# The first FFN's first chunks computed without the shift, which is added to them later

## The chip, the cores and the metric

One Trainium2 (trn2) chip; the kernel runs on one core. The metric is the device time of one execution in microseconds (us). A core has TensorE (PE; its weight loads are listed as PEld), VectorE (DVE), ScalarE (ACT), GpSimd (POOL) and SyncE (SP). Here SP and POOL issue nearly all loads, which land in SBUF through 16 shared DMA engines. Each engine, and each queue of loads, works through its instructions in order.

## The reference

One step of a two-layer network on T = 384 tokens (128 context, 256 latent) of width 1024. Each layer is a half-step FFN, a mixer, and a second half-step FFN, so the kernel has six stages s = 0..5; s = 0 and 3 are the first FFNs. What matters here is the start of the first FFN:

```python
mod = silu(cond) @ w_ada + b_ada          # nine vectors of 1024 per layer, one set per kind of token
shift, scale, gate = mod[0], mod[1], mod[2]
h = rmsnorm(x, g[0]) * (1.0 + scale) + shift
g, u = split(h @ w_ffn_in)                # w_ffn_in: 1024 x 5632 (2816 for g, 2816 for u)
x = x + 0.5 * gate * ((silu(g) * u) @ w_ffn_out)
```

cond is one vector for the context tokens and one for the latent tokens, so shift and scale have two columns. rmsnorm multiplies each token by one number r. Thus h @ w = r * ((x * g[0] * (1 + scale)) @ w) + shift @ w, and the last product is one number per output column and kind of token.

## The kernel before, in words

All matrices are fp32. Each is split in a high part (a cast on ACT, L470) and the rest (a subtraction on DVE, L471), and each product takes three matmuls: high x high, high x low, low x high (`mm3`, L474; lines L475, L476, L477). Activations lie feature by feature: xT is 8 k-blocks of 128 features by 384 tokens.

**An FFN** (`ffn`, L562) has 22 chunks f of 128 columns of g and 128 of u. A chunk takes two slabs (`ffn_slab`, L555; `wslab`, L460) of 512 KB, one for k-blocks 0 to 3 and one for 4 to 7, each loaded by two issues of 256 KB on SP's queue (L466). It runs 24 mm3 products of 384 columns into pg and 24 matmul triples in the same manner into pu, 48 matmuls in all, then SiLU, the product with u and a split into aH and aL. After the 22 chunks the out part (po) multiplies them by w_ffn_out. The slabs' raw tiles have 5 buffers (tag X), the high parts 4 and the low parts 4; the chunks' sums have 4 banks of PSUM (tag pw).

**Two forms of the left factor.** `mod_chunk` (L502) makes h itself for one k-block, split in hH and hL: on DVE two products t = xT * am * r (L508) and two subtractions (L512), on ACT two additions of the shift. `raw_chunk` (L520) makes x * am only, am = g[0] * (1 + scale), without r, and puts the two columns of the shift behind the 384 tokens (L526, L531), so that the same matmuls yield shift @ w in columns 384 and 385 (TR = 386). A chunk that uses raw factors multiplies by r afterwards and adds those two numbers (L581 to L587). N_RAW says how many chunks of each FFN do that; for s = 0 it is the first two, since r is late.

**The modulation vectors.** `ada_first` (L297) forms shift and scale of stage 0, in four calls of 256 columns each: four loads of 512 KB on SP's queue (L309), 32 small matmuls with 32-column weights (each seen as two passes in the trace), a copy on ACT, a transposition on PE, an addition, am. It is called before everything else of the FFN, with two `raw_chunk` calls after each call, and the slabs of f = 0 and f = 1 are loaded after the calls i = 0 (k-blocks 0 to 3) and i = 2 (k-blocks 4 to 7). Its tiles come from the tags K (3 buffers) and X. All other vectors, 1024 columns each, are groups (s, p) of a stream (`Stream`, L394; `ada_group`, L343): p = 0 shift, 1 scale, 2 gate. A group has 8 steps; a step loads 512 KB on POOL's queue (L354; tag AX, 3 buffers) and either multiplies on PE (4 matmuls, L368) or accumulates on DVE (two instructions of 128x1024, L360 and L362; at the group's end 8 matmuls with a block of ones add up the partitions, L378, then a transposition, L379). The order is (0,2), (1,0), (1,1), (1,2), ...; ADA_F says how many DVE steps are spread over an FFN's chunks and over its out part, for s = 0 20 and 12.

**The order of the work.** A list scheduler places each engine's instructions ahead of time: by default in program order, a ready instruction before one that is not; slabs' splits get a lead of 60 instructions. `behind` puts one instruction after another on its engine. `late_loads` (L221) issues 18 small parameter loads on POOL's queue once the last raw factor is there (L531).

Of the kernel before, what the change touches and what calls it, by code (L numbers as in the profile page):

```python
# [11 lines left out]
F32 = mybir.dt.float32  # L12
# [24 lines left out]
ADA_F = [[20, 12], None, [24, 12], [20, 16], None, [8, 0]]  # L37
ADA_M = [14, 0]

N_RAW = [2, None, 2, 2, None, 2]  # L40
# [44 lines left out]
def hybrid_step_kernel(  # L85
# [211 lines left out]
    def ada_first(i):  # L297
# [3 lines left out]
        for q in range(2):  # L301
            xs = []
            for g in range(2):
                if (i + q) % 2 == 0:
                    x = kp.tile([P, HALF_K, 256], F32, name="adax", tag="K")
                else:
                    x = wp.tile([P, HALF_K, 256], F32, name="adax", tag="X")
                rows = w_ada[0, q * HALF_K * P : (q + 1) * HALF_K * P, g * D + 256 * i : g * D + 256 * i + 256]
                nc.sync.dma_start(x, rows.rearrange("(k p) n -> p k n", p=P))  # L309
                xs.append(x)  # L310
            for kk in range(HALF_K):
                k = q * HALF_K + kk
                for g in range(2):
                    for j in range(2):
                        r0 = 64 * g + 32 * j
                        mm(
                            bank[r0 : r0 + 32, 0:P],
                            sc[:, k, :],
                            xs[g][:, kk, j * P : (j + 1) * P],
                            start=(k == 0),  # L320
                            stop=(k == KD - 1),
                        )
        sb = mp.tile([P, 512], F32, name="adasb", tag="adasb", bufs=1)
        nc.scalar.copy(sb[:, 0:P], bank[:, 0:P])
        ps = PS("psada", "p2")
        nc.tensor.transpose(ps[:, 0:P], sb[:, 0:P], ident)
        m = slice(2 * i, 2 * i + 2)
        V.tensor_tensor(
            md[:, 0:16, :].rearrange("p (g m) c -> p g m c", g=2)[:, :, m, :],
            ps[:, 0:P].rearrange("p (g j c) -> p g j c", g=2, j=2)[:, :, :, 0:2],  # L330
            vC[0][:, 0:16].rearrange("p (g m) -> p g m", g=2)[:, :, m].unsqueeze(3).to_broadcast([P, 2, 2, 2]),
# [3 lines left out]
            am[:, m, :],  # L335
            md[:, KD + 2 * i : KD + 2 * i + 2, :],
            1.0,
            g_norm(0, 0)[:, m].unsqueeze(2).to_broadcast([P, 2, 2]),
# [4 lines left out]
    def ada_group(s, p, on_dve):  # L343

        l, i = divmod(s, 3)
# [3 lines left out]
        bias = vC[l][:, i * 24 + KD * p : i * 24 + KD * p + KD]  # L349
        accs = [K5(f"ada{c}") for c in range(2)] if on_dve else None  # L350
        bank = None if on_dve else PS("adaps", "pa")
        for k in range(KD):
            x = wp.tile([P, 1024], F32, name="adax", tag="AX", bufs=3)
            nc.gpsimd.dma_start(x, w_ada[l, k * P : (k + 1) * P, c0 : c0 + D])  # L354
            if on_dve:
                x = x.rearrange("p (h n) -> p h n", h=2)
                for c in range(2):
                    w = sc[:, k, c : c + 1]
# [6 lines left out]
            else:  # L365
                x = x.rearrange("p (m a j) -> p a m j", m=KD, a=4)
                for a in range(4):
                    ins = mm(bank[32 * a : 32 * a + 32, 0:256], sc[:, k, :], x[:, a], start=(k == 0), stop=(k == KD - 1))  # L368
                    if norm_last["pe"] is not None:
                        behind(ins, norm_last["pe"])  # L370
            yield
        sb = mp.tile([P, 512], F32, name="adasb", tag="adasb", bufs=1)
        if on_dve:
# [5 lines left out]
            V.transpose(out=sb, in_=bank)  # L379
            src = sb.rearrange("p (c m j) -> p m c j", c=2, m=KD)[:, :, :, 0]  # L380
# [11 lines left out]
    norm_last = {"dve": None, "pe": None}  # L392
# [28 lines left out]
    ada = Stream([(0, 2)] + [(s, p) for s in range(1, 3 * DEPTH) for p in range(3)])  # L421
# [98 lines left out]
    def raw_chunk(s, k):  # L520
# [873 lines left out]
```

## Time and profile before

| | us |
|---|---|
| median of 3 runs (1579.45 to 1580.15) | 1580.09 |
| the profiled execution, device time | 1580.6 |
| its span, first to last instruction | 1578.8 |
| share of PE in the chain that ended last | 88% |
| mean granted TensorE clock | 0.991 |

The span is what the trace covers; 1.8 us of the profiled execution lie around it, and it is 0.5 us over the median. A row of a view by lines reads: line, engine, operation, out<-in by the program's names, shape, count | busy us, mean ns of one | idle time before. A row in order of time reads: start, duration (of the whole merged piece), engine, line, operation, count, and in brackets the idle time before it and what ended it. The duration of one matmul in these rows is its latency; successive ones start about half as far apart, because they are pipelined.

### The profile page before, as it was taken

The page shows a single profiled execution, that of the slowest core. Times are in us where ns is not written, and L with a number is a line of the kernel's source. Part 1 is how long each engine was busy: PE and PEld are TensorE (multiplying, and loading weights), DVE is VectorE, ACT ScalarE, POOL GpSimd, SP SyncE. Part 2 cuts the span into 40 slices and gives each one's busy share as a digit, 9 for nine tenths or more (in the row PEclk, how much of TensorE's full clock was granted, in tenths as well). Part 3 has the DMA queues.
Part 4 walks back from the last instruction along what each step waited for, and adds up shares of the span by engine and source line. Part 5 has one row for each costly group of instructions (what it writes and reads, how often), then busy time and mean ns, then how long its engine had stood idle before and what let it go on. Part 6 is the DMA issues. An engine that isn't in the chain of part 4 may idle for free.

```text
span 1578.8 us, 24260 instructions
## 1 busy us (share of the span) xinstructions
PE 1527.9 (97%) x9118; PEld 1441.2 (91%) x9118; DVE 1113.6 (71%) x2068; ACT 746.6 (47%) x1376; POOL 103.4 (7%) x194
## 2 busy tenths in 40 slices
PE   7999999999889999999999999999978999999998
PEld 5899999998668999999999999999857699999998
DVE  5888586587677988578578866777967789443332
ACT  4533332469577633333363333325975864333221
POOL 1202010001100001001000200110000000000000
PEclk9999999999999999999999999999989999999999
DMA  9978576523531587566537866674231046444341
GB/s 304 248 205 228 158 231 196 147 80 115 185 106 37 146 245 211 161 207 225 171 97 215 238 187 193 203 238 121 64 92 37 15 134 201 130 117 128 116 145 35
DMA packets 291034, 249.02 MB, mean 158 GB/s; under 512 B 11554, under 2 KB 273159, under 8 KB 290917
## 3 DMA queue, kind: packets, MB, share of 16 engines
q1 hardware_dynamic: 270224, 175.94, 38.2%
q0 software_dynamic: 20368, 71.34, 14.8%
q8 instruction: 71, 1.16, 0.3%
q14 instruction: 47, 0.38, 0.1%
q10 hardware_dynamic: 324, 0.20, 0.1%
HBM read 245.17 MB, written 2.27 MB: 157 GB/s over the span
## 4 chain that ended last, share of the span: by engine, by line
PE 88%; DVE 4%; ACT 4%; issue 2%; DMA 1%; POOL 0%; ACTq 0%; DVEq 0%; POOLq 0%
PE po L475 9%; PE po L476 9%; PE po L477 9%; PE pg L475 8%; PE pg L477 8%; PE pg L476 8%; PE pu L475 8%; PE pu L477 8%; PE pu L476 8%; PE psw L476 1%; PE psg L891 1%; PE psw L475 1%; PE psw L477 1%; PE adaps L378 1%; ACT gate L143 1%
## 5 line engine op out<-in xcount | busy, mean ns | idle before, releaser
L471 DVE TENSOR_TENSOR wl<-wx,wh 128x1024 fp32r<-128x1024 f32 (+2 forms) x332 | 385.4, 1163 | 302.8 <-ACT wh L470 294.3
L470 ACT CAST wh<-wx 128x1024 fp32r<-128x1024 f32 (+2 forms) x332 | 333.2, 1005 | 448.5 <-PE po L476 237.3
L362 DVE SCALAR_TENSOR_TENSOR ada<-adax,sc,ada 128x1024 f32<-128x1024 f32 x196 | 244.2, 1280 | 17.8 <-DMA adax<-in_w_ada_dram 17.4
L475 PE MATMUL po<-aH,wh 128*128 128x384 f32 x704 | 239.7, 341 | 0.0
L477 PE MATMUL po<-aH,wl 128*128 128x384 f32 x704 | 237.7, 338 | 0.0
L476 PE MATMUL po<-aL,wh 128*128 128x384 f32 x704 | 237.2, 337 | 0.0
L475 PE MATMUL pg<-hH,wh 128*128 128x384 f32 x640 | 216.9, 339 | 0.0
L475 PE MATMUL pu<-hH,wh 128*128 128x384 f32 x640 | 216.2, 338 | 0.0
L477 PE MATMUL pg<-hH,wl 128*128 128x384 f32 x640 | 215.9, 337 | 0.2 <-DVE wl L471 0.2
L477 PE MATMUL pu<-hH,wl 128*128 128x384 f32 x640 | 215.6, 337 | 0.0
L476 PE MATMUL pu<-hL,wh 128*128 128x384 f32 x640 | 215.5, 337 | 0.0
L476 PE MATMUL pg<-hL,wh 128*128 128x384 f32 x640 | 215.4, 337 | 0.0
L143 ACT ACTIVATE sg<-pg 128x384 f32<-128x384 f32 x80 | 39.4, 493 | 206.5 <-PE pg L477 206.5
L475 PEld LDWEIGHTS po<-aH,wh 128*128 128x128 f32 x704 | 132.4, 188 | 3.9 <-issue 2.1
L476 PEld LDWEIGHTS po<-aL,wh 128*128 128x128 f32 x704 | 132.2, 188 | 0.5 <-issue 0.5
L477 PEld LDWEIGHTS po<-aH,wl 128*128 128x128 f32 x704 | 132.2, 188 | 0.0
L354 POOL DMA_DIRECT2D adax<-in_w_ada_dram x128 | 68.1, 533 | 892.3 <-DVE ada L360 466.5
L475 PEld LDWEIGHTS pg<-hH,wh 128*128 128x128 f32 x640 | 120.2, 188 | 2.5 <-issue 2.1
L477 PEld LDWEIGHTS pg<-hH,wl 128*128 128x128 f32 x640 | 120.1, 188 | 0.6 <-DVE wl L471 0.5
L476 PEld LDWEIGHTS pg<-hL,wh 128*128 128x128 f32 x640 | 120.2, 188 | 0.0
L475 PEld LDWEIGHTS pu<-hH,wh 128*128 128x128 f32 x640 | 120.2, 188 | 0.0
L477 PEld LDWEIGHTS pu<-hH,wl 128*128 128x128 f32 x640 | 120.1, 188 | 0.0
(327 smaller groups left out, 2425.9 us busy)
## 6 DMA issues: line engine op xcount, KB each, us to landing
wx<-in_w_ffn_in_dram SPq DMA_DIRECT2D x352, 256.0 KB, 4.1
adax<-in_w_ada_dram POOLq DMA_DIRECT2D x128, 512.0 KB, 4.9
wx<-in_w_ffn_out_dram SPq DMA_DIRECT2D x80, 512.0 KB, 3.9
wx<-in_w_in_dram SPq DMA_DIRECT2D x28, 512.0 KB, 3.8
adax<-in_w_ada_dram SPq DMA_DIRECT2D x16, 512.0 KB, 7.7
wx<-in_w_ffn_out_dram SPq DMA_DIRECT2D x16, 256.0 KB, 3.3
wx<-in_w_out_dram SPq DMA_DIRECT2D x8, 512.0 KB, 3.9
wx<-in_w_out_dram SPq DMA_DIRECT2D x16, 256.0 KB, 2.7
```

The lines of the kernel that those rows point to most:

```text
L143: ins = nc.scalar.activation(out, in_, func, **kw)
L354: nc.gpsimd.dma_start(x, w_ada[l, k * P : (k + 1) * P, c0 : c0 + D])
L362: ins = V.scalar_tensor_tensor(accs[c], x, w, accs[c], ALU.mult, ALU.add)
L378: mm(bank[32 * a : 32 * a + 32, 256 * c : 256 * c + 256], cm(C_ONE, n1=32), x[:, a], start=True, stop=True)
L470: nc.scalar.copy(h[:, 0:nk, 0:ncol], x[:, 0:nk, 0:ncol])
L471: V.tensor_tensor(lo[:, 0:nk, 0:ncol], x[:, 0:nk, 0:ncol], h[:, 0:nk, 0:ncol].bitcast(F32), ALU.subtract)
L475: mm(out, wh, xh, start=first, stop=False)
L476: mm(out, wh, xl, start=False, stop=False)
L477: last_mm[0] = mm(out, wl, xh, start=False, stop=last)
L891: mm(ps[:, 0:TG], wg[:, wi, :], xcs[ch], start=True, stop=True)
```

## The change

For s = 0, `ada_first` loads and forms the scale only: two loads per call in place of four, 16 matmuls in place of 32. `raw_chunk` no longer writes the shift's two columns for s = 0; `raw_cols` does that later. The shift becomes group (0,0) of the stream, on PE, and its first load on POOL's queue waits for the last matmul of `ada_first`; the three loads that POOL issued at the very start are no longer there. Chunks f = 0 to 3 ("late" chunks) run on raw factors over the 384 tokens alone; DVE multiplies their two sums by r into tiles of SBUF that are kept. The 8 steps of (0,0) stand two by two after pg and after pu of f = 2 and f = 3. Behind f = 3 come `raw_cols` for the 8 k-blocks, `late_loads` and the 8 calls of `mod_chunk`. Chunk f = 4 uses the raw factors with the two columns, f = 5 to 21 use h. Group (0,1), which had been the scale's, now forms shift @ w_ffn_in for the columns of f = 0 to 3: 8 steps on DVE, each loading 512 KB of w_ffn_in on POOL's queue, then 8 summing matmuls and a transposition; `late_shift` adds the result to the kept tiles, does SiLU, product and split. The DVE steps, 28 in place of 20, are spread over f = 5 to 21.

```diff
-ADA_F = [[20, 12], None, [24, 12], [20, 16], None, [8, 0]]
+ADA_F = [[28, 12], None, [24, 12], [20, 16], None, [8, 0]]
...
-N_RAW = [2, None, 2, 2, None, 2]
+N_RAW = [1, None, 2, 2, None, 2]
+
+N_LATE = 4
...
@@ -299,63 +301,73 @@
-            xs = []
-            for g in range(2):
-                if (i + q) % 2 == 0:
-                    x = kp.tile([P, HALF_K, 256], F32, name="adax", tag="K")
-                else:
-                    x = wp.tile([P, HALF_K, 256], F32, name="adax", tag="X")
-                rows = w_ada[0, q * HALF_K * P : (q + 1) * HALF_K * P, g * D + 256 * i : g * D + 256 * i + 256]
-                nc.sync.dma_start(x, rows.rearrange("(k p) n -> p k n", p=P))
-                xs.append(x)
+            if q == 0:
+                x = kp.tile([P, HALF_K, 256], F32, name="adax", tag="K")
+            else:
+                x = wp.tile([P, HALF_K, 256], F32, name="adax", tag="X")
+            rows = w_ada[0, q * HALF_K * P : (q + 1) * HALF_K * P, D + 256 * i : D + 256 * i + 256]
+            nc.sync.dma_start(x, rows.rearrange("(k p) n -> p k n", p=P))
...
+        norm_last["scale"] = ins
...
-        nc.tensor.transpose(ps[:, 0:P], sb[:, 0:P], ident)
-        m = slice(2 * i, 2 * i + 2)
+        nc.tensor.transpose(ps[:, 0:64], sb[0:64, 0:P], cm(C_ID, 0, 64, 0, 64))
...
+        late = (s, p) == (0, 1)
+        on_dve = on_dve or late
+        first_load = []
         for k in range(KD):
             x = wp.tile([P, 1024], F32, name="adax", tag="AX", bufs=3)
-            nc.gpsimd.dma_start(x, w_ada[l, k * P : (k + 1) * P, c0 : c0 + D])
+            if late:
+                win = w_ffn_in[0, 0, k * P : (k + 1) * P, :].rearrange("p (g n) -> p g n", g=2)
+                nc.gpsimd.dma_start(x.rearrange("p (g n) -> p g n", g=2), win[:, :, 0 : N_LATE * P])
+            else:
+                ins = nc.gpsimd.dma_start(x, w_ada[l, k * P : (k + 1) * P, c0 : c0 + D])
+                if (s, p) == (0, 0):
+                    if k == 0:
+                        tc.add_manual_dep(ins.ins, norm_last["scale"].ins.name, sync, reason="order of the loads")
+                        first_load.append(ins)
+                    else:
+                        behind(ins, first_load[0])
             if on_dve:
                 x = x.rearrange("p (h n) -> p h n", h=2)
                 for c in range(2):
-                    w = sc[:, k, c : c + 1]
+                    w = md[:, k, c : c + 1] if late else sc[:, k, c : c + 1]
...
                 for a in range(4):
                     ins = mm(bank[32 * a : 32 * a + 32, 0:256], sc[:, k, :], x[:, a], start=(k == 0), stop=(k == KD - 1))
-                    if norm_last["pe"] is not None:
-                        behind(ins, norm_last["pe"])
+                    behind(ins, last_mm[0])
...
+            if late:
+                late_shift(sb.rearrange("p (c g f j) -> p c g f j", c=2, g=2, f=N_LATE))
+                return
...
-    ada = Stream([(0, 2)] + [(s, p) for s in range(1, 3 * DEPTH) for p in range(3)])
+    ada = Stream([(s, p) for s in range(3 * DEPTH) for p in range(3)])
...
         h, lo = LT("rH", (P, TR), F32R), LT("rL", (P, TR), F32R)
         for j, sl in SEG:
             act(h[:, sl], xT[:, k, sl], AF.Copy, scale=am[:, k, j : j + 1])
-        V.tensor_copy(h[:, T:TR], md[:, k, :])
         for j, sl in SEG:
             V.scalar_tensor_tensor(
                 lo[:, sl], xT[:, k, sl], am[:, k, j : j + 1], h[:, sl].bitcast(F32), ALU.mult, ALU.subtract
             )
+        raws.setdefault(s, []).append((h, lo))
+        if s:
+            raw_cols(s, k)
+
+    def raw_cols(s, k):
+        md, _ = mods[s]
+        h, lo = raws[s][k]
+        V.tensor_copy(h[:, T:TR], md[:, k, :])
         norm_last["raw"] = V.tensor_tensor(lo[:, T:TR], md[:, k, :], h[:, T:TR].bitcast(F32), ALU.subtract)
-        raws.setdefault(s, []).append((h, lo))
...
+    late_acts = []
+
+    def late_shift(b):
+
+        for f in range(N_LATE):
+            sg, su_ = late_acts[f]
+            for j, sl in SEG:
+                act(sg[:, sl], sg[:, sl], AF.Silu, bias=b[:, j, 0, f, 0:1])
+            for j, sl in SEG:
+                V.scalar_tensor_tensor(sg[:, sl], su_[:, sl], b[:, j, 1, f, 0:1], sg[:, sl], ALU.add, ALU.mult)
+            late_acts[f] = split(sg, "a", pool=LT)
...
-            raw = f < N_RAW[s]
-            xs, n = (raws[s], TR) if raw else (hs, T)
+            late = s == 0 and f < N_LATE
+            raw = not late and f < N_RAW[s] + (N_LATE if s == 0 else 0)
+            xs, n = (raws[s], T) if late else (raws[s], TR) if raw else (hs, T)
             for ps, o in ((pg, 0), (pu, P)):
                 for k in range(KD):
                     h, lo = slabs[k // HALF_K]
                     w0 = slice(o, o + P)
                     kk = k % HALF_K
-                    mm3(ps[:, 0:n], h[:, kk, w0], lo[:, kk, w0], *xs[k], k == 0, k == KD - 1)
+                    xh, xl = (x[:, 0:n] for x in xs[k])
+                    mm3(ps[:, 0:n], h[:, kk, w0], lo[:, kk, w0], xh, xl, k == 0, k == KD - 1)
+                if late and f >= 2:
+                    ada.step(2)
+            if late:
+                late_acts.append((S("sg"), S("su")))
+                for x, ps in zip(late_acts[f], (pg, pu)):
+                    V.tensor_tensor(x, ps[:, 0:T], r, ALU.mult)
+                acts.append(None)
+                if f == N_LATE - 1:
+                    for k in range(KD):
+                        raw_cols(0, k)
+                    late_loads(norm_last["raw"])
+                    hs = [mod_chunk(0, k, r) for k in range(KD)]
+                continue
...
-            if f >= 2:
+            f0 = N_LATE + 1 if s == 0 else 2
+            if f >= f0:
                 n = ADA_F[s][0]
-                ada.step(n * (f - 1) // (KF - 2) - n * (f - 2) // (KF - 2), True)
+                ada.step(n * (f + 1 - f0) // (KF - f0) - n * (f - f0) // (KF - f0), True)
...
         ada.until(s, 2)
+        acts[0 : len(late_acts)] = late_acts
+        late_acts.clear()
...
-    hs = [mod_chunk(0, k, r) for k in range(KD)]
-    late_loads(norm_last["raw"])
+    hs = None
```

## Rows read from the trace of the kernel before

**Rows 1.** The page: busy time by engine, and the chain by engine

```profile
PE 1527.9 (97%) x9118; PEld 1441.2 (91%) x9118; DVE 1113.6 (71%) x2068; ACT 746.6 (47%) x1376; POOL 103.4 (7%) x194
...
PE 88%; DVE 4%; ACT 4%; issue 2%; DMA 1%; POOL 0%; ACTq 0%; DVEq 0%; POOLq 0%
```

**Rows 2.** Busy time by stretch: us, each engine's busy time (instructions), granted clock, DMA share, GB/s

```profile
0.00:22.54 22.54, 12.83 (x98) 8.58 (x98) 8.41 (x24) 9.01 (x18) 4.10 (x9) 1.00 0.99 319
22.54:58.58 36.04, 31.58 (x291) 23.97 (x292) 24.55 (x79) 19.26 (x42) 3.11 (x6) 0.91 0.91 260
58.58:229.60 171.02, 170.79 (x993) 168.49 (x993) 137.10 (x194) 67.94 (x93) 24.22 (x45) 1.00 0.76 212
229.60:329.00 99.40, 99.40 (x580) 95.93 (x579) 62.12 (x105) 36.55 (x59) 4.24 (x8) 1.00 0.57 170
```

**Rows 3.** PE in order of time: start, us, line, tile, count

```profile
22.54 0.45 PE L475 MATMUL pg<-rH,wh 128*128 128x386 f32 x1
...
50.47 1.07 PE L316 MATMUL ada<-adax,sc 128*32 128x128 f32 x28
...
53.91 0.45 PE L475 MATMUL pg<-rH,wh 128*128 128x386 f32 x1 [0.44 <-ACT rH L143]
...
58.58 0.34 PE L475 MATMUL pg<-hH,wh 128*128 128x384 f32 x1
```

**Rows 4.** PE in order of time, end of the first FFN's chunks

```profile
230.27 0.33 PE L475 MATMUL po<-aH,wh 128*128 128x384 f32 x1
```

**Rows 5.** DMA from 0 to 58.58 us: bytes; issues, KB each, us to landing

```profile
DMA packets 19247, 16.54 MB, mean 282 GB/s; under 512 B 793, under 2 KB 18469, under 8 KB 19242
...
adax<-in_w_ada_dram SPq DMA_DIRECT2D x16, 512.0 KB, 7.7
...
adax<-in_w_ada_dram POOLq DMA_DIRECT2D x3, 512.0 KB, 8.5
```

**Rows 6.** What SP's queue waited for, 0 to 80 us: total, times, longest

```profile
SPq L466 <- DVE wl L471: 19.7, 8, 8.3
SPq L309 <- PE ada L316: 8.2, 3, 4.3
```

**Rows 7.** PE by line, 0 to 58.58 us: count, busy us, mean ns

```profile
L316 PE MATMUL ada<-adax,sc 128*32 128x128 f32 x256 | 13.6, 314 | 2.2 <-DVE acc L439 1.3 <-DMA adax<-in_w_ada_dram 0.9
```

**Rows 8.** Chain of waits: one group's summing on PE

```profile
127.08 1.00 PE adaps L378 x16
```

**Rows 9.** PE in order of time, modulation steps on PE in the first mixer

```profile
403.27 0.64 PE L368 MATMUL adaps<-adax,sc 128*32 128x256 f32 x8 [3.67 <-DMA adax<-in_w_ada_dram]
```

**Rows 10.** Busy time by stretch around two dips of the granted clock

```profile
40.00:45.00 5.00, 2.62 (x28) 1.70 (x32) 4.80 (x13) 3.45 (x8) 0.00 (x0) 0.81 1.10 346
45.00:50.00 5.00, 5.00 (x30) 3.74 (x22) 1.37 (x4) 0.91 (x2) 0.00 (x0) 0.50 1.20 293
...
400.00:405.00 5.00, 0.64 (x8) 0.16 (x8) 4.44 (x12) 3.52 (x7) 1.17 (x3) 1.00 0.98 345
405.00:410.00 5.00, 4.84 (x20) 2.48 (x21) 1.25 (x5) 1.82 (x7) 1.63 (x3) 0.66 1.06 363
```

**Rows 11.** POOL's loads of w_ada: ns of one issue; us from issue to landing

```profile
L354 POOL DMA_DIRECT2D adax<-in_w_ada_dram x128: 530/530/657, 2.5 to 1333.6; - x128
...
DMA to landing us min/median/max: 3.7/4.9/9.7
```

**Rows 12.** DVE by line and shape, 20 to 58.58 us

```profile
L512 DVE SCALAR_TENSOR_TENSOR hL<-ht,md,hH 128x256 fp32r<-128x256 f32 x8 | 3.9, 482 | 0.3 <-ACT hH L143 0.3
...
L512 DVE SCALAR_TENSOR_TENSOR hL<-ht,md,hH 128x128 fp32r<-128x128 f32 x8 | 2.8, 350 | 0.2
...
L526 DVE CAST rH<-md 128x2 fp32r<-128x2 f32 x8 | 1.3, 164 | 0.0
```

**Rows 13.** DVE by line, 58.58 to 227 us

```profile
L362 DVE SCALAR_TENSOR_TENSOR ada<-adax,sc,ada 128x1024 f32<-128x1024 f32 x43 | 53.8, 1281 | 7.7 <-DMA adax<-in_w_ada_dram 7.6
L471 DVE TENSOR_TENSOR wl<-wx,wh 128x1024 fp32r<-128x1024 f32 x42 | 51.2, 1222 | 21.8 <-ACT wh L470 21.7
```

More of the change, by code (lines that the diff above doesn't have):

```diff
@@ L311, in ada_first @@
+            rows = w_ada[0, q * HALF_K * P : (q + 1) * HALF_K * P, D + 256 * i : D + 256 * i + 256]
+            nc.sync.dma_start(x, rows.rearrange("(k p) n -> p k n", p=P))
             for kk in range(HALF_K):
                 k = q * HALF_K + kk
[L313 to L322, printed above, removed]
+                for j in range(2):
+                    ins = mm(
+                        bank[32 * j : 32 * j + 32, 0:P],
+                        sc[:, k, :],
+                        x[:, kk, j * P : (j + 1) * P],
+                        start=(k == 0),
+                        stop=(k == KD - 1),
+                    )
@@ L323, in ada_first @@
+        norm_last["scale"] = ins
         sb = mp.tile([P, 512], F32, name="adasb", tag="adasb", bufs=1)
-        nc.scalar.copy(sb[:, 0:P], bank[:, 0:P])
+        nc.scalar.copy(sb[0:64, 0:P], bank[0:64, 0:P])
         ps = PS("psada", "p2")
-        nc.tensor.transpose(ps[:, 0:P], sb[:, 0:P], ident)
-        m = slice(2 * i, 2 * i + 2)
+        nc.tensor.transpose(ps[:, 0:64], sb[0:64, 0:P], cm(C_ID, 0, 64, 0, 64))
+        m = slice(KD + 2 * i, KD + 2 * i + 2)
         V.tensor_tensor(
-            md[:, 0:16, :].rearrange("p (g m) c -> p g m c", g=2)[:, :, m, :],
-            ps[:, 0:P].rearrange("p (g j c) -> p g j c", g=2, j=2)[:, :, :, 0:2],
-            vC[0][:, 0:16].rearrange("p (g m) -> p g m", g=2)[:, :, m].unsqueeze(3).to_broadcast([P, 2, 2, 2]),
+            md[:, m, :],
+            ps[:, 0:64].rearrange("p (j c) -> p j c", j=2)[:, :, 0:2],
+            vC[0][:, m].unsqueeze(2).to_broadcast([P, 2, 2]),
@@ L334, in ada_first @@
         V.scalar_tensor_tensor(
-            am[:, m, :],
-            md[:, KD + 2 * i : KD + 2 * i + 2, :],
+            am[:, 2 * i : 2 * i + 2, :],
+            md[:, m, :],
             1.0,
-            g_norm(0, 0)[:, m].unsqueeze(2).to_broadcast([P, 2, 2]),
+            g_norm(0, 0)[:, 2 * i : 2 * i + 2].unsqueeze(2).to_broadcast([P, 2, 2]),
             ALU.add,
@@ L390, in ada_group @@
             V.tensor_scalar(md[:, m, :], md[:, m, :], 0.5, None, op0=ALU.mult)
-    norm_last = {"dve": None, "pe": None}
+    norm_last = {"dve": None}
     class Stream:
@@ L496, in norm_stat @@
         for n_, sq in enumerate(acc["sq"]):
-            norm_last["pe"] = mm(ps[:, 0:T], cm(C_ONE), sq, start=(n_ == 0), stop=(n_ == len(acc["sq"]) - 1))
+            mm(ps[:, 0:T], cm(C_ONE), sq, start=(n_ == 0), stop=(n_ == len(acc["sq"]) - 1))
         return rsqrt_newton(ps[:, 0:T], T, 1.0 / D, acc["t"])
```

## The prediction, made before the changed kernel ran

> **What bounds the kernel now.** I read the page first: PE is busy for 97% of the span and holds 88% of the chain that ended last [rows 1], so a saving counts only where PE itself does less, or where PE waits. The busy times by stretch show where it waits. From 58.58 us on, PE is busy in 170.79 of 171.02 us of the first FFN's remaining chunks, and then without a gap through the out part; before 58.58 us it is not, and the DMA engines are (share 0.99 and 0.91, 319 and 260 GB/s) [rows 2]. PE in order of time gives the marks: the first FFN matmul starts at 22.54 us, the last call of `ada_first` ends at 51.54 us, the matmuls that hang on it begin at 53.91 us, and f = 2 starts at 58.58 us [rows 3]; the out part begins at 230.27 us [rows 4]. So f = 0 and 1, two chunks of 48 matmuls, end only at 58.58 us. By then 16.54 MB have been moved, of which 16 loads of 0.52 MB on SP's queue for shift and scale (8.4 MB) and three on POOL's for the gate (1.6 MB); one takes 7.7 us and 8.5 us to land [rows 5]. The stretch is bound by bytes, with some turns of buffers: SP's queue waited 19.7 us for the slabs' splits and 8.2 us for the small matmuls [rows 6].
>
> A chunk's pace follows from the marks. Between 58.58 and 230.27 us lie 171.7 us: 20 chunks, two summings of a group on PE (L378; 1.00 us each [rows 8], 1.2 us with the slower start of the matmuls behind), and 0.8 us of small things. So a chunk takes (171.7 - 2.4 - 0.8) / 20 = 8.42 us.
>
> **The change, part by part.** All sums are made on the profiled execution (span 1578.8 us, 1580.6 us in all, 0.5 us over the median of 1580.09); the difference is carried to the median. I compute E, the time at which f = 0 and 1 are done, and then the start of the out part.
>
> *Removed: half of `ada_first`'s loads and matmuls, and POOL's three early loads.* Ahead of the last scale load there were 8.4 MB of modulation, 2.1 MB of slabs, 1.6 MB of tokens and 1.6 MB from POOL; now there are 4.2 + 2.1 + 1.6 = 7.9 MB. At 319 GB/s [rows 2] that is 25 us; with the turns of buffers that SP keeps [rows 6] I take 30 us. From the last call's end to its first matmul took 53.91 - 51.54 = 2.4 us, and the two k-blocks behind it are 24 matmuls of 0.175 us, 4.2 us: loads allow E = 37. PE itself allows less. From 22.54 to 58.58 us it was busy for 31.58 us [rows 2]. Off that comes half of the small matmuls of three calls: of 256 passes in all [rows 7] 192 lie here, 28 take 1.07 us [rows 3], so half of them, 96, are 3.7 us. Also off comes what the half clock cost: from 45 to 50 us the granted clock was 0.50, the lower level of 1.2 GHz, after a stretch in which PE had been busy for 2.62 of 5 us [rows 10]; some 3 us. 24.9 us stay. The first FFN matmul comes sooner by between 1.2 us (half of one call's 64 passes) and 8 us (2.6 MB less ahead of it, 1.6 from POOL and 1.0 of the first call's shift, at 319 GB/s); the transpositions and squares of x stay ahead of it, so I take 4, near the lower end: 18.5 us. That gives 18.5 + 24.9 = 43.4, and with 0.6 us of waits left of the 4.5 us there are now, E = 44. The ends are 39.4 (8 us sooner, no wait) and 52 (22.54 + 24.9 + 4.5, nothing sooner, every wait stays).
>
> *Moved to PE's full stretch: the shift.* Group (0,0) is 8 steps of 8 passes. 16 passes cost 1.00 us [rows 8], 1.2 us with the restart, and the steps come two by two, in four places: 4 x 1.2 = 4.8 us. They were hidden under loads; now nothing hides them.
>
> *Moved to POOL's queue: the shift's loads.* The first three wait for the last scale matmul, some 31 us, and have until E + 4.2 = 48. The other five wait for one of three buffers, so each is issued only when the step three places earlier has run. POOL issues one in 0.53 us, and it lands in 3.7 to 9.7 us, median 4.9 [rows 11]. PE consumes two in 5.4 us. At the median, step 3 is issued at 48.2 and lands at 53.1, when PE reaches it (53.6); the others come out alike. I take 0.7 us of waits; ends 0 (all at 3.7) and 6 (rival D).
>
> *Added: a wait ahead of f = 4.* It needs the last step, a transposition and an addition on DVE and `raw_cols`, two instructions of 0.16 us [rows 12] per k-block. PE has no other work left, as h for f = 5 needs the same shift. No such wait is in the trace. Below it stand two such instructions, 0.3 us, above it the longest wait of PE for a modulation load, 3.67 us [rows 9]; nearest is `ada_first`'s own chain of copy, transposition, addition and cast, 2.4 us [rows 3]. I take 2.2.
>
> *Moved: `mod_chunk` from the idle start into f = 4.* Per k-block DVE has two subtractions of 0.35 and 0.48 us [rows 12] and two products of the same shapes: 1.66 us, 13.3 us for eight by durations, and some 10.6 us as neighbours overlap at their ends. Together with `raw_cols` (2 us) and the split of f = 5's slabs (2 x 1.2 [rows 13]) DVE has 15 us to do from the start of f = 4 to the last k-block of f = 5's pg, 12.6 us later; some 2 us of products can be done ahead, since they don't need the shift. I take 1 us of waits for PE; ends 0 and 4.
>
> *Added: group (0,1) on DVE, 16 instructions of up to 1.28 us [rows 13], 1.2 from start to start, and `late_shift`.* On PE that is one more summing, 1.2 us. On DVE it goes beside PE: a chunk costs DVE 3.3 us (two splits, product, split of a), 28 steps over 17 chunks are 1.65 x 2.4 = 4.0 us, together 7.3 of 8.42. So it fits, with little room; what slips goes to the out part, where DVE is busy for 62 of 99 us [rows 2]. I take 0.5 us. `late_loads`' 18 issues now come 10 us later, but their first user is behind f = 8. Behind POOL's queue, then, stand only loads of group (0,1), which DVE can't use before `mod_chunk` is done. The later stages keep their modulation: 40 steps in place of 32 cover the additional group.
>
> *Sum.* The out part starts at E + 20 x 8.42 + 3 x 1.2 + 0.8 + 4.8 + 0.7 + 2.2 + 1 + 0.5 = 44 + 182 = 226.0, against 230.3: 4.3 us sooner. What follows is the same and PE-bound. 1580.1 - 4.3 = 1575.8 us.
>
> **A rule against the rows.** POOL's issue of a modulation load took 530 ns in the median and 657 at most over 128 issues [rows 11], most of them while DVE was full (137 of 171 us [rows 2]). The Trainium skill, SBUF — State Buffer, section "SBUF: two separate sides", says that a load issued by GpSimd can be held up until a VectorE instruction in a two-port mode ends, and gives some 620 ns alone against 3100 ns beside one. By that, each turn of a shift buffer would be about 2.5 us longer, and rival D would come true; the rows of this kernel don't show it so far.
>
> **The rivals.**
> - *B, the start gives more.* The first matmul comes 6 us sooner and the later waits stay near their lower ends: E = 41, 2 us less behind it. Then 1580.1 - 9.3 = 1570.8. For it: everything ahead of the first matmul is loads. Against: x must still be transposed and squared.
> - *C, VectorE becomes the bound.* DVE's 15 us around f = 5 can't be brought forward, then `late_params` and group (0,1) find it full, and PE waits for wl or for a free bank: 3 to 5 us more than I took. 1578.8 to 1580.8, about 1579.5. For it: DVE had 137 us of work in 171 us and now has more in less. Against: PE was idle for only 0.23 us there [rows 2].
> - *D, slower: the three buffers of the shift's loads throttle PE.* If a load takes the 8.5 us of POOL's first three [rows 5] in place of 4.9, step 3, issued at 48.2, lands at 56.7, when PE has been waiting since 53.6, and step 7 makes it wait as long again: 6.2 us in all, 5.5 more than taken. The second wait runs into that ahead of f = 4, some 5 us with hardly a matmul; behind the wait of 3.67 us, in a stretch where PE was busy for 0.64 of 5 us, the granted clock was 0.66 [rows 9, 10], which here costs 2 to 3 us. Together 1580.1 - 4.3 + 5.5 + 2.5 = 1583.8. It decides once a turn takes over about 6 us; slower than before from about 8. For it: slabs and shift together want 250 + 124 GB/s. Against: the median, and that the slabs are loaded up to two chunks ahead.
> - *E, the start does not shrink as the bytes do.* Buffers, not bytes, turn SP's queue, and E is 48 to 52: 1579.8 to 1583.8. For it: 28 us of waits in SP's queue [rows 6]. Against: DMA share 0.91 to 0.99.
>
> **How the numbers follow.** Chances: forecast 0.41, B 0.13, C 0.14, D 0.13, E 0.19. A measurement of this kernel can tell about 0.2%, 3.2 us, from no change. Faster by more than that (under 1576.9): nearly all of the forecast's and B's chance, a little of the others, 0.53. Within: the forecast's upper edge 0.03, most of C, two thirds of E and some of D, 0.29. Slower (over 1583.3): most of D, a third of E, C's tail, 0.18. Both signs have much of the chance, so the forecast's own range is 1572 to 1579. The range for 8 in 10 reaches from B's lower half to just past D: 1569.5 to 1584.5.
>
> **What would show it.** Right: f = 2 starts at about 44 us; no granted clock of 0.5 before it; four pieces of L368 of about 1 us in f = 2 and 3 with waits under 1 us; a gap of about 2 us ahead of f = 4; the out part at 226 us, and equal distances behind it. Wrong: f = 2 beyond 48 us; waits for adax of 3 us in f = 2 or 3; idle PE before pg or pu of f = 5 to 12 with DVE as the releaser.

## The result, and the profile after

The changed kernel takes 1596.66 us in the median of 4 runs (1595.46 to 1599.45), the kernel before 1579.77 us on the same chip (4 runs, 1578.22 to 1580.15). The ratio is 1.0111, 95% interval 1.0094 to 1.0129: **slower by 16.9 us**, where a time under that of the kernel before was forecast, and outside both predicted ranges.

First the page of the changed kernel, busy time and the chain by engine; it answers to [rows 1].

```profile
PE 1540.6 (96%) x9070; PEld 1448.3 (91%) x9070; DVE 1134.9 (71%) x2094; ACT 745.5 (47%) x1379; POOL 114.0 (7%) x210
...
PE 85%; issue 5%; DVE 4%; ACT 3%; DMA 2%; POOL 0%; ACTq 0%; DVEq 0%; POOLq 0%
```

PE has 48 instructions fewer and is busy for 12.7 us longer: about half of that is slower clock (the mean granted clock is 0.987, before 0.991, which over the span is some 6 us, an estimate from these two). The span is 18.9 us longer, so 6.2 us are new idle time. Where both lie is seen in the busy times by stretch, cut at PE's marks: first FFN matmul, start of f = 2, f = 4 and f = 6, out part. The row of the first mixer follows. The columns are those of [rows 2]. (A chunk's 48 matmuls are 8 `mm3` products into pg and 8 into pu.)

```profile
13.63:27.36 13.73, 11.98 (x109) 7.50 (x105) 9.13 (x21) 7.54 (x17) 0.00 (x0) 1.00 1.10 326
27.36:47.70 20.34, 20.34 (x132) 18.56 (x132) 13.43 (x28) 8.46 (x15) 1.72 (x3) 1.00 0.85 254
47.70:74.84 27.14, 23.28 (x161) 19.38 (x160) 9.87 (x18) 5.24 (x5) 4.80 (x8) 0.94 0.69 212
74.84:100.05 25.21, 21.02 (x96) 19.75 (x97) 14.84 (x53) 10.04 (x20) 9.04 (x17) 0.86 0.53 133
100.05:238.85 138.80, 138.80 (x820) 136.01 (x820) 131.70 (x187) 59.80 (x88) 22.87 (x39) 1.00 0.82 238
...
335.63:540.19 204.56, 189.00 (x1168) 154.97 (x1168) 157.21 (x438) 144.97 (x349) 15.19 (x29) 0.97 0.34 104
```

What the reader is to see: f = 0 and 1 are done at 47.7 us in place of 58.58 [rows 3], so the start did win 10.9 us in these two profiles. Then f = 2 and 3 take 27.1 us and f = 4 and 5 take 25.2 us, where two chunks took 16.8; and that is where PE idles (3.9 and 4.2 us) and the clock falls (0.94 and 0.86). From f = 6 to the out part PE is full again. PE in order of time gives the pieces:

```profile
27.36 0.45 PE L489 MATMUL pg<-rH,wh 128*128 128x384 f32 x1
...
65.17 0.87 PE L380 MATMUL adaps<-adax,sc 128*32 128x256 f32 x8 [1.78 <-DMA adax<-in_w_ada_dram]
...
74.84 0.41 PE L489 MATMUL pg<-rH,wh 128*128 128x386 f32 x1 [2.08 <-DVE rH L551]
...
86.77 0.44 PE L489 MATMUL pg<-hH,wh 128*128 128x384 f32 x1 [1.67 <-ACT hH L145]
...
89.08 0.50 PE L490 MATMUL pg<-hL,wh 128*128 128x384 f32 x1 [1.69 <-DVE hL L526]
...
96.64 0.44 PE L489 MATMUL pg<-hH,wh 128*128 128x384 f32 x1 [0.84 <-ACT hH L145]
...
238.85 0.34 PE L489 MATMUL po<-aH,wh 128*128 128x384 f32 x1
```

The out part starts 8.6 us later than in [rows 4]. The second part of the loss is far behind the edit's place: the first mixer, 196.4 us before, takes 204.6. Together that is 16.8 us, close to the 16.9 us between the medians, but a profile shows one execution: that of after is 2.8 us over its median, and its second mixer is 2.4 us longer than that of before, with the same longest waits. The first FFN differs by more. Two of the runs below have unchanged code there and give a second profile of it: in e4 (as before) f = 2 starts at 54.93 and the out part at 226.62 us, in e2 (as after) at 45.70 and 234.91. So the start won 9.2 us in that pair, the out part came 8.3 us later, and a single mark is good to some 4 us.

ACT in order of time shows why h came late. Its rows read as PE's do:

```profile
71.62 1.04 ACT L484 CAST wh<-wx 128x1024 fp32r<-128x1024 f32 x1 [1.06 <-PE pu L490]
82.83 1.05 ACT L484 CAST wh<-wx 128x1024 fp32r<-128x1024 f32 x1 [10.16 <-PE pu L490]
84.96 1.04 ACT L484 CAST wh<-wx 128x1024 fp32r<-128x1024 f32 x1 [1.08 <-PE pu L490]
85.92 2.18 ACT L145 ACTIVATE hH<-ht,md 128x128 fp32r<-128x128 f32 x6
```

The shift was complete at 74.5 us (md, L398). But ACT stood idle for 10.2 us, from 72.7 to 82.8, because next in its order came the casts of a slab for f = 6, which had to wait until f = 4 gave a buffer back; hH stood behind them. DVE did likewise: it waited for the sums of f = 4 and then for `gains`, and with it stood wl and hL.

```profile
81.08 0.16 DVE L557 COPY rb<-pg 128x2 f32<-128x2 f32 x1 [5.28 <-PE pg L491]
83.58 0.20 DVE L1333 TENSOR_SCALAR gains<-gains 128x64 f32<-128x64 f32 x1 [2.34 <-DMA gains<-in_diff_qk_norm_dram]
85.21 0.26 DVE L1333 TENSOR_SCALAR gains<-gains 128x192 f32<-128x192 f32 x1 [1.44 <-DMA gains<-in_mla_qk_norm_dram]
```

### The profile page after: what moved, and what is told of

Same layout as the page of the kernel before. It is cut to its first block, busy times and chain, and to the rows that moved or that the text cites. A ratio compares the mean times of both kernels' runs of the same rounds, so it can differ in the third digit from the quotient of the medians.

```text
span 1597.7 us, 24217 instructions
## 1 busy us (share of the span) xinstructions
PE 1540.6 (96%) x9070; PEld 1448.3 (91%) x9070; DVE 1134.9 (71%) x2094; ACT 745.5 (47%) x1379; POOL 114.0 (7%) x210
## 4 chain that ended last, share of the span: by engine, by line
PE 85%; issue 5%; DVE 4%; ACT 3%; DMA 2%; POOL 0%; ACTq 0%; DVEq 0%; POOLq 0%
PE po L489 9%; PE po L490 9%; PE po L491 9%; PE pg L489 7%; PE pg L491 7%; PE pg L490 7%; PE pu L489 7%; PE pu L491 7%; PE pu L490 7%; DMA adax<-in_w_ada_dram 1%; PE psg L941 1%; ACT gate L145 1%; PE psw L490 1%; PE psw L489 1%; PE adaps L389 1%
## 5 line engine op out<-in xcount | busy, mean ns | idle before, releaser
L489 PE MATMUL pg<-hH,wh 128*128 128x384 f32 x616 | 209.1, 339 | 2.5 <-ACT hH L145 2.5
L490 PE MATMUL pg<-hL,wh 128*128 128x384 f32 x616 | 208.1, 338 | 1.7 <-DVE hL L526 1.7
L491 PE MATMUL pg<-hH,wl 128*128 128x384 f32 x616 | 208.2, 338 | 0.0
L489 PE MATMUL pu<-hH,wh 128*128 128x384 f32 x616 | 207.9, 337 | 0.0
L491 PE MATMUL pu<-hH,wl 128*128 128x384 f32 x616 | 207.8, 337 | 0.0
L490 PE MATMUL pu<-hL,wh 128*128 128x384 f32 x616 | 207.6, 337 | 0.0
L489 PEld LDWEIGHTS pg<-hH,wh 128*128 128x128 f32 x616 | 115.8, 188 | 6.0 <-ACT hH L145 3.1
L490 PEld LDWEIGHTS pg<-hL,wh 128*128 128x128 f32 x616 | 115.9, 188 | 2.3 <-DVE hL L526 2.2
L490 PEld LDWEIGHTS pu<-hL,wh 128*128 128x128 f32 x616 | 115.9, 188 | 0.0
L491 PEld LDWEIGHTS pu<-hH,wl 128*128 128x128 f32 x616 | 115.8, 188 | 0.0
```

The costliest lines, as they stand in the source:

```text
L489: mm(out, wh, xh, start=first, stop=False)
L490: mm(out, wh, xl, start=False, stop=False)
L491: last_mm[0] = mm(out, wl, xh, start=False, stop=last)
```

## The experiments

Two theories were set up at first. **Theory 1**: in the FFN, the loss comes from `late_loads`, which is now called ahead of `mod_chunk`; the planner places what depends on its 18 issues, and hH and hL, late in each engine's order. **Theory 2**: in the mixer, the loss comes from one line of the diff: in `ada_group` every group on PE, not only (0,0), is now bound behind the last matmul of an FFN (`last_mm[0]`) in place of the norm's (`norm_last["pe"]`), so the first mixer's modulation steps can no longer fill its gaps.

**e1, `late_loads` behind `mod_chunk`** (changed kernel):

```diff
-                    late_loads(norm_last["raw"])
                     hs = [mod_chunk(0, k, r) for k in range(KD)]
+                    late_loads(norm_last["raw"])
```

> The changed kernel with one line moved: late_loads stands behind the eight mod_chunk calls instead of ahead of them. Theory 1 (the tiles of late_loads and of h share one tag and are handed out in program order, so h waits until POOL has issued its 18 loads, 76.1 to 86.5 us): the additions of the shift on ACT start some 10 us sooner, right behind raw_cols, ahead of the next slab's cast; the waits of PE in f = 5 (1.67, 1.69 and 0.84 us) and the half clock at 89 to 93 us go, and the whole gets 5 to 7 us shorter than the changed kernel's 1596.7, about 1590.5. Rival 1 (DVE and ACT have too much to do around f = 5, whatever the order): within 2 us of 1596.7.

1588.66 us (1586.69 to 1589.41), ratio to before 1.006 [1.004, 1.008]: 8.0 us less than the changed kernel, more than the 5 to 7 expected. No wait for hH or hL is left; the first of h's matmuls comes at 80.52 us (86.77 in the changed kernel), f = 6 at 88.93 and the out part at 227.62. The first mixer still takes 204.5 us. Theory 1 holds for the place of the call. Why that place matters (hH's tiles come from the same pool as the tiles that `late_loads` fills, and the planner hands them out in program order) is read from the code; no run isolates it.

**e2, the other groups bound as before** (changed kernel):

```diff
-                    behind(ins, last_mm[0])
+                    behind(ins, last_mm[0] if (s, p) == (0, 0) else norm_last["pe"])
```

(and `norm_stat` notes its last matmul again).

> The changed kernel, with the modulation matmuls of all groups but (0,0) bound behind the last matmul of the norm's sum, as before, and no longer behind the last mm3. Theory 2 (the new binding keeps the mixer's modulation matmuls and their loads out of the first mixer's gap): they come back into the gap ahead of the transpositions of cl, the first mixer is 7 to 9 us shorter, and the whole about 1588.5. Rival 2 (the mixer lost its 8 us to something that comes from the first FFN, as later loads or another state of the clock): the first mixer stays at 204.6 us, the whole within 2 us of 1596.7. The start of the first FFN is as in the changed kernel by both.

**e4, that binding alone, in the kernel before**:

```diff
-                    if norm_last["pe"] is not None:
-                        behind(ins, norm_last["pe"])
+                    behind(ins, last_mm[0])
```

> The kernel before with that one part of the change alone: the modulation matmuls on PE are bound behind the last mm3 instead of behind the norm's sum. Theory 2: the first mixer gets 7 to 9 us longer (196.4 to about 204.5), everything ahead of it is the same, the whole about 1588. Rival 2: within 1.5 us of 1579.8.

e2: 1587.06 us (1585.49 to 1588.19), 1.0051 [1.0031, 1.007], 9.6 us less than the changed kernel; its first mixer takes 196.1 us. e4: 1588.72 us (1585.51 to 1590.71), 1.006 [1.0036, 1.0084], 8.7 us more than the kernel before on the same chip (1579.99), with a first mixer of 205.0 us. This one edit does it, alone. What PE waited for in the first mixer shows how; first the kernel before, then e4 (total, times, longest):

```profile
PE adaps L368 <- DMA adax<-in_w_ada_dram: 6.0, 3, 3.7
...
PE psk L1013 <- DVE yc L755: 0.6, 1, 0.6
```

```profile
PE pst L988 <- ACT cl L143: 6.5, 1, 6.5
PE psk L1012 <- DVE yc L754: 2.4, 1, 2.4
PE po L474 <- DVE ya L1178: 2.2, 1, 2.2
```

The first of the mixer's modulation matmuls, before and e4, in order of time:

```profile
387.36 1.48 PE L368 MATMUL adaps<-adax,sc 128*32 128x256 f32 x18
```

```profile
447.29 1.07 PE L368 MATMUL adaps<-adax,sc 128*32 128x256 f32 x16
```

In the kernel before, PE does modulation matmuls where the mixer's own chain (cl, ya, yc) is late, and pays 6.0 us for their loads. Bound behind the FFN's last matmul they come later (the first mixer begins at 326.9 us in before and at 323.2 in e4, so the first stands 60 us into it in place of 124), the three gaps stay empty, 11.1 us, and the work is still to be done. Why the planner places them so much later was not tried. The trace of before had shown the price: in its second mixer, which has no modulation steps, PE waits for the same three:

```profile
PE pst L989 <- ACT cl L143: 6.5, 1, 6.5
PE po L475 <- DVE ya L1179: 2.2, 1, 2.2
PE psk L1013 <- DVE yc L755: 2.0, 1, 2.0
```

**e3, both undone** (e1's and e2's edits together):

> Both edits together. Theories 1 and 2: the gains add, 12 to 16 us, about 1582.5, still not under the kernel before, because f = 2 starts at 47.7 us and the shift's steps, one wait and the wait ahead of f = 4 stay. Rivals: what the single edits don't give is not given here; if only one of them is right, 1588 to 1591.

1579.25 us (1576.84 to 1581.89, 10 runs), 1.0001 [0.999, 1.0012]. The two gains add up (17.4 us, more than the 12 to 16 expected) and nothing is left of the loss, but nothing of the 10.9 us at the start either. So a **theory 3** was needed: the shift itself eats the lead. In e3 f = 2 starts at 46.71 us and f = 4 at 73.99, near the 75.91 of the kernel before. Between them lie two chunks (16.8 us), four pieces of the shift (4.8), waits of 1.91 and 2.09 us, and half-clock matmuls behind each. The profile of e3 is that of the slowest of its ten runs. In e1, e2 and e12, which have the same work on PE there, the clock does not fall and f = 4 starts at 71.94, 70.47 and 72.38 us; in e4, with the code of before, at 72.26. So the lead is gone by f = 4 there too, but the half clock is no fixed part of its price.

**e5, the shift on DVE** in place of PE:

```diff
-                if late and f >= 2:
-                    ada.step(2)
+                if late and f in (1, 2):
+                    ada.step(2, True)
```

> The kernel of e3_both, with the eight steps of the shift on VectorE (in f = 1 and 2) in place of TensorE (in f = 2 and 3). Theory 3: what the start wins (f = 0 and 1 done at 47.7 us in place of 58.6) is eaten by the shift itself: four pieces of 1.07 us on TensorE and their restarts (4.9 us), a wait of 1.8 us for a buffer turn of the loads, a wait of 2.1 us ahead of f = 4, and the half clock behind both (some 3 us). On VectorE, which was busy for 10 of 27 us there, the pieces become one summing of 1.2 us and the buffer wait with its half clock goes: about 6.5 us off 1579.25, so 1572 to 1574; the wait ahead of f = 4 stays near 2 us. Rival (VectorE's turn): its instructions wait in order for their loads and hold the reading of pg and pu behind them, so that TensorE waits for a bank: 1579 or more, with idle TensorE ahead of f = 3. Rival (the shift's time is set by its loads): f = 4 starts at the same 74 us whatever engine sums it, 1578 to 1580.

1577.96 us (1576.00 to 1581.69, 12 runs), 0.9994 [0.9985, 1.0004]: f = 4 starts at 66.11 us, 7.9 sooner than in e3, but by the medians only 1.3 us of that reach the end, which the intervals can't tell from nothing. The expected 1572 to 1574 was missed. Half of theory 3 holds (the lead was spent there), its price at the end does not. The wait ahead of f = 4, which was to stay near 2 us, is 0.82. The busy times by stretch, e3 and then e5, show the next bound:

```profile
60.00:80.00 20.00, 16.01 (x92) 13.60 (x91) 10.40 (x38) 6.18 (x13) 6.59 (x12) 0.83 0.79 236
80.00:100.00 20.00, 20.00 (x115) 20.00 (x115) 18.67 (x31) 11.29 (x18) 6.75 (x13) 1.00 0.73 176
```

```profile
60.00:80.00 20.00, 16.41 (x95) 13.55 (x95) 19.30 (x55) 10.08 (x20) 10.50 (x19) 1.00 0.57 157
80.00:100.00 20.00, 20.00 (x107) 20.00 (x106) 18.01 (x25) 8.72 (x12) 2.21 (x3) 0.92 0.88 233
```

In e3 DVE (third number) is half idle while PE waits; in e5 it is full, 19.3 of 20 us, and PE waits for a split of a slab that stands behind nearly all of `mod_chunk`:

```profile
78.81 0.44 PE L491 MATMUL pg<-hH,wl 128*128 128x384 f32 x1 [1.90 <-DVE wl L485]
```

So **theory 4**: around f = 4 and 5 DVE is the bound, and what counts is the order of its work.

**e9, the shift's columns, `mod_chunk` and `late_loads` called earlier**, between pg and pu of f = 3 of e5:

> The kernel of e5_shift_dve, with the eight calls of raw_cols, mod_chunk and late_loads called between pg and pu of f = 3 in place of behind f = 3, so that they stand earlier on VectorE and ScalarE. Theory 3: the wait ahead of f = 4 (2.1 us) and the waits for hH and hL at the first matmuls of f = 5 (1.7 us) come from their place in the order and not from the work: both fall under 0.7 us, with the half clock behind them, and the time is 3 to 5 us under that of e5_shift_dve, 1568 to 1570. Rival (VectorE is full there): the 15 us that VectorE has to do around f = 4 and 5 can't come earlier, the wait moves to wl of f = 4 or f = 5, and the time is that of e5_shift_dve within 1.5 us.

1581.08 us (1579.06 to 1584.95, 11 runs), 1.001 [1.0002, 1.0019]: 3.1 us worse than e5. The two waits that it was to shorten were those of the changed kernel; e5 has 0.82 us ahead of f = 4 and none for hH or hL. In e9 PE waited 1.74 us ahead of f = 4 and 3.75 us for DVE's reading of a chunk's sums (L631, at 80.79 us), which stood behind the work for h from 69.7 to 79.5 us:

```profile
81.48 0.41 PE L489 MATMUL pg<-hH,wh 128*128 128x384 f32 x1 [3.75 <-DVE sg L631]
```

My expectation failed. Its rival, that VectorE is full there, holds in kind; but it had put the wait at wl and the time within 1.5 us of e5's.

**e6, e10 and e11**: two chunks (f = 4 and 5) on raw factors, so that h is wanted one chunk later, with three places for the work on h.

```diff
-N_RAW = [1, None, 2, 2, None, 2]
+N_RAW = [2, None, 2, 2, None, 2]
```

e6 has e5's order. e10 calls `raw_cols` between pg and pu of f = 3 and all of `mod_chunk` behind f = 4. e11 splits it, k = 0 to 3 behind f = 3 and k = 4 to 7 behind f = 4:

```diff
+                if f == N_LATE - 1:
+                    hs = [mod_chunk(0, k, r) for k in range(HALF_K)]
...
+            if s == 0 and f == N_LATE:
+                hs += [mod_chunk(0, k, r) for k in range(HALF_K, KD)]
+                late_loads(norm_last["raw"])
```

> The kernel of e5_shift_dve, with two chunks in place of one (f = 4 and 5) on x and the shift's columns, so that h is wanted first by f = 6. Theory 4: what e5_shift_dve won by f = 4 (66.1 us against 74.0) is lost between f = 4 and 6 because VectorE is full there: from 64.4 to 83 us it works without a gap at the shift's columns, the 32 instructions of mod_chunk and the splits of f = 4 to 6, in that order, and TensorE waits for a split (2.4 us) and runs at the half clock behind it. A chunk later for h alone does not change the order: the splits of f = 5 still stand behind mod_chunk, so the same wait for wl comes, 1577 to 1579. Rival (h is late, not VectorE): the wait goes with the need for h, 1574 to 1575.

> As e6_shift_dve_raw2, with raw_cols called between pg and pu of f = 3, and all eight calls of mod_chunk and late_loads called behind f = 4; the two scalings of gains on VectorE stand behind the last instruction of mod_chunk. Theory 4: VectorE's queue is relieved ahead of f = 4 and 5 (no wait for wl, none ahead of f = 4), and h for f = 6 starts only at about 76 us and takes 11 to 13 us, so a wait of 2 to 4 us stands ahead of or in f = 6: 1576 to 1578. Rival (the loss was waits alone): no wait over 1 us from f = 3 to f = 7, 1572 to 1574.

> As e10_raw2_mid, with mod_chunk of k = 0 to 3 called behind f = 3 and that of k = 4 to 7 behind f = 4. Theory 4: VectorE's 11 us for h are spread over two chunks in which it has 17 us, with the splits between them, so no wait over 1 us is left from f = 4 to f = 7, and no half clock; the lead of 8 to 9 us at f = 4 is kept but for the additional summing (1.2 us): 1572 to 1574. Rival (VectorE is full for longer than two chunks, as group (0,1) comes right behind): the waits move to f = 6 and 7, 1576 to 1579.

e6: 1578.98 us (0.9999 [0.9989, 1.0009]), with the same wait for wl (1.9 us). e10: 1577.76 us (0.9993 [0.9983, 1.0003]); that wait is gone, 1.75 us stand ahead of f = 4, and in f = 6, when h is made, PE waits for a split again:

```profile
91.15 0.44 PE L491 MATMUL pg<-hH,wl 128*128 128x384 f32 x1 [1.25 <-DVE wl L485]
```

**e11: 1574.63 us (1573.07 to 1576.66, 10 runs), 0.9969 [0.9957, 0.998]**, 5 us under the kernel before: it beats both, and is 0.6 us over its expected range. Of its waits the one ahead of f = 4 is left (1.74 us), behind that none:

```profile
60.00:80.00 20.00, 18.14 (x110) 16.50 (x110) 19.49 (x53) 10.83 (x20) 10.46 (x19) 1.00 0.86 225
80.00:100.00 20.00, 20.00 (x116) 20.00 (x115) 19.73 (x33) 9.47 (x16) 2.20 (x3) 1.00 0.55 157
```

DVE is as full as in e5 and e6 (19.30 and 19.19 of the first 20 us). Against e5 a second chunk is on raw factors too, but that alone gains nothing, as e6 shows (1578.98 us); against e6 only the order differs, and it is worth 4.4 us.

**e12, e11 with the shift on PE**, the fourth corner:

> The kernel of e11_raw2_halves with the shift's eight steps on TensorE again, in f = 2 and 3, and raw_cols behind f = 3, as in e3_both; two rows of the mixer's tables on VectorE are tied behind f's later work as their neighbours are. With e3_both (shift on TensorE, old order: 1579.25), e5_shift_dve (VectorE, old order: 1577.96) and e11_raw2_halves (VectorE, new order: 1574.63) it makes the fourth corner. Theory 4: the lead that the start wins is spent by the shift on TensorE before f = 4 begins (about 74 us, as in e3_both), and the order of VectorE behind it can only save the 1 to 2 us that e3_both loses between f = 4 and 6; so 1577 to 1579.5. Rival (the order of VectorE alone makes the gain): within 1 us of e11_raw2_halves, 1574 to 1576.

1578.78 us (1577.31 to 1582.82, 10 runs), 0.9996 [0.9985, 1.0006]. The time lies where theory 4 had put it, with f = 4 at 72.38 in place of about 74 us. Its profiled execution has a second mixer of 196.6 us, like that of after, where the others have 194.2 to 194.8; whether all its runs have that is open. PE's marks follow (us; start of f = 2, f = 4, f = 6 and the out part, then the time from f = 2 to the out part, the median, and what the profiled execution is over the median). In the table the new order includes the second chunk on raw factors:

| kernel | f = 2 | f = 4 | f = 6 | out | f = 2 to out | median | profile over it |
|---|---|---|---|---|---|---|---|
| before | 58.58 | 75.91 | 92.73 | 230.27 | 171.7 | 1579.77 | 0.8 |
| e4 (as before here) | 54.93 | 72.26 | 89.09 | 226.62 | 171.7 | 1588.72 | -3.2 |
| after | 47.65 | 74.84 | 100.05 | 238.85 | 191.2 | 1596.66 | 2.8 |
| e2 (as after here) | 45.70 | 70.47 | 95.95 | 234.91 | 189.2 | 1587.06 | -1.6 |
| e1 | 46.54 | 71.94 | 88.93 | 227.62 | 181.1 | 1588.66 | -2.0 |
| e3 (PE, old order) | 46.71 | 73.99 | 92.50 | 231.19 | 184.5 | 1579.25 | 2.6 |
| e12 (PE, new order) | 47.12 | 72.38 | 89.43 | 228.49 | 181.4 | 1578.78 | 1.1 |
| e5 (DVE, old order) | 46.46 | 66.11 | 88.18 | 226.87 | 180.4 | 1577.96 | -0.7 |
| e6 (DVE, old order, 2 raw) | 47.36 | 66.82 | 87.39 | 226.08 | 178.7 | 1578.98 | -0.1 |
| e11 (DVE, new order) | 46.83 | 67.29 | 84.34 | 223.37 | 176.5 | 1574.63 | 0.1 |

e1 and e3 have the same code here and differ by 3.4 us, in one profile each, so differences of that size in the table say little, and the medians decide (before has 1579.4 to 1580.0 us on the chips of these runs). By them the shift on DVE is worth 1.3 us in the old order and 4.2 in the new one, the new order 0.5 us with the shift on PE and 3.3 with it on DVE. Of the four corners only e11 can be told from the kernel before: by these runs the gain needs both.

## Why the prediction was wrong

The prediction's marks were f = 2 at 44 us and the out part at 226.0; its sum gives f = 4 at 68.5 and f = 6 at 86.4. Set against the row of after, it came out late by 3.7 us at f = 2, 6.3 at f = 4, 13.7 at f = 6 and 12.9 at the out part, and by 8.2 us more in the first mixer: 1575.8 + 12.9 + 8.2 = 1596.9 us, measured 1596.66, closer than such marks are good for. In e2's profile of the same code it is late by 1.7, 2.0, 9.6 and 8.9 us. In both, most of what is lost in the FFN is lost in f = 4 and 5, and the rest of the loss lies in the mixer. Step by step:

- **"What follows is the same and PE-bound"** failed outright; this is the largest error of kind. The last rows of the diff's `ada_group` rebind every group on PE, not (0,0) alone. The edit stood in the quoted diff and got no cost. e4 shows 8.7 us and e2 9.6. It would have been found by asking, of each changed line, which other calls run it: ADA_M sends 14 steps of the first mixer there, and [rows 9] are such steps.
- **"`late_loads`' 18 issues come 10 us later, but their first user is behind f = 8"** costed the issues and missed the order. They come 20.6 us later (the first at 76.09 us, before at 55.47), and their first user, the scaling of `gains` on DVE, ran at 83.58 us, in f = 4. Being called ahead of `mod_chunk` they left hH and hL behind f = 6's casts on ACT, and `gains` ahead of wl on DVE. For f = 4 and 5, 1 us of waits was forecast over 16.8; measured are 25.2 (25.5 in e2): 4.2 us idle and 4.2 us more busy time, at a granted clock of 0.86. e1 gives back 8.0 us.
- **E = 44** was 47.7 (45.7 to 47.1 in e1, e2, e3 and e12), inside its ends (39.4 to 52), and that was partly luck. The term "first FFN matmul 4 us sooner" had the wrong sign: it came at 27.36, 4.8 us later. PE had no room to give there. In the kernel before, the 8.41 us ahead of the first FFN matmul were full of transpositions, small matmuls and the norm's sum, as this stretch shows (columns of [rows 2]):

```profile
14.13:22.54 8.41, 8.41 (x81) 5.46 (x81) 4.17 (x11) 3.67 (x9) 0.00 (x0) 1.00 1.14 323
```

  In the changed kernel PE is busy from 13.63 to 47.7 us but for 1.75 us, so bytes no longer bound this stretch. Nor did half the small matmuls take half the time. In the changed kernel 16 passes last as long as 28 did in [rows 3], where they went to four blocks of 32 rows and now go to two; over the start they are busy for 10.7 us in place of 13.6 [rows 7], where the prediction took off 3.7 us for three of the four calls:

```profile
22.27 1.07 PE L313 MATMUL ada<-adax,sc 128*32 128x128 f32 x16
```

  The 24.9 us behind the first FFN matmul fell to 20.3 and made up for half of the lateness. One reason is that 96 of the 128 passes now lie ahead of it; no run tells what the rest is. The 3 us that the prediction took off for the half clock [rows 10] were those of one execution: in e4's profile, with the same code, the granted clock is 1.00 there, and f = 2 starts at 54.93:

```profile
21.60:54.93 33.33, 28.96 (x292) 22.03 (x292) 24.39 (x79) 19.36 (x42) 3.12 (x6) 1.00 1.00 288
```

  Rival E (48 to 52) missed narrowly, and for another reason than buffers.
- **The shift on PE, 4.8 us**: right; three pieces of 1.07 us, and 0.64 + 0.87. **The wait ahead of f = 4, 2.2 us**: measured 2.08. **The shift's loads, 0.7 us**: 1.78. Not priced by the forecast was the half clock behind both waits; rival D had it, at 2 to 3 us. f = 2 and 3 took 27.1 us against 24.5; in e1, e2 and e12, where the clock did not fall, they took 25.4, 24.8 and 25.3.
- **The loads' rule of rival D** did not bite. The Trainium skill, SBUF — State Buffer, section "SBUF: two separate sides", would have POOL's issue held up beside a VectorE instruction in a two-port mode. No hold-up shows here: in e5 five of the eight issues of the shift's loads run while DVE is busy for 20.00 of 20 us (40 to 60 us), and the eight take 548 ns in the mean, near the 530 of [rows 11]. Whether any of DVE's instructions there is in a two-port mode no run shows, so the rule itself is not tested. ([rows 2], which the prediction read as a full DVE, has it busy for 137 of 171 us, 80%.)

```profile
L360 POOL DMA_DIRECT2D adax<-in_w_ada_dram x8 | 4.4, 548 | 48.7 <-PE ada L313 30.3 <-DVE ada L374 12.7 <-DMA adax<-in_w_ada_dram 5.6
```

- **Group (0,1) on DVE, 1.7 us**: from f = 6 to the out part it takes 138.8 us against 137.5; 1.2 us for the additional summing, and PE is never idle. The fear of rival C for f = 6 to 21 was groundless, but its other half, that DVE's work around f = 5 can't be brought forward, fits what e5, e9 and e6 ran into once the first two faults were gone.

Without the two overlooked effects the forecast would still have been too good: e3 stands at 1579.25, not 1575.8. The idea was worth what was forecast only with the shift on DVE and the order of e11.

## What to carry to other kernels

Read a diff line by line for who else runs a changed line: a binding written for one group moved another stage's filler work out of its gaps, and that cost 8 to 9 us, twice what the change was to win. When engines work in order, price a moved call by what it now stands ahead of and what is then held behind it, not by its own duration. And when a wait has been taken from the busiest engine, look which engine is full at that place next: here DVE, where the order alone decided between 1579.0 us (e6) and 1574.6 (e11). And before a stretch of one profile is read to a microsecond, look at a second profile of the same code: here two of them differed by 4 us.

## What the runs showed of the hardware that was not expected

A wait's price is not its length. In e3 PE waited 2.09 us ahead of f = 4, and soon after it ran at the lower level, 1.2 GHz, though it was busy all the time; the chunk f = 4 took 10.1 us, and 10.3 in the changed kernel, behind a wait of 2.08. In e1, e2 and e12 PE waits as long at the same place, 2.08 to 2.09 us, behind the same work, and the granted clock stays at 1.00: f = 4 takes 8.6 to 8.7 us. In e11 the wait was 1.74 us and the clock stayed too. The stretches behind the waits, e3 first:

```profile
74.62:77.83 3.21, 3.21 (x11) 3.21 (x11) 3.21 (x14) 1.91 (x6) 2.38 (x5) 0.50 0.92 303
```

Then e1, e2, e12 and e11:

```profile
71.94:80.52 8.58, 8.58 (x48) 8.58 (x49) 8.58 (x38) 6.35 (x17) 5.73 (x11) 1.00 0.89 227
```

```profile
70.47:79.18 8.71, 8.71 (x48) 8.39 (x48) 1.12 (x14) 1.18 (x2) 5.64 (x11) 1.00 0.86 222
```

```profile
72.38:80.93 8.55, 8.55 (x48) 8.55 (x49) 5.09 (x26) 5.80 (x12) 5.05 (x10) 1.00 0.91 223
```

```profile
67.29:75.86 8.57, 8.57 (x48) 8.57 (x49) 8.57 (x30) 3.77 (x8) 6.72 (x13) 1.00 0.93 209
```

So the price of this wait changed from one profile to the next: some 1.5 us of half clock or none. What decides is not shown. The profiles differ in the wait for a load some 8 us earlier, 1.78 us (after) and 1.91 (e3) against 1.53 (e1), 0.90 (e2) and 1.40 (e12), but that was not tried apart. A forecast can give such a half clock only as a chance.

Half as many small matmuls are not half as long: 16 passes of `ada_first` into two blocks of 32 rows lasted 1.07 us, as did 28 into four.
